# Routing spread over more units and begun during the queries, with its index picking in 16 bits

## The chip, the cores and the metric

One Trainium2 chip, one core. The metric is device time in microseconds of one execution. The kernel before ran three times: 2064.03 us median, 2062.64 lowest, 2065.06 highest.

## The reference

Two layers act on 256 latent tokens of width 1024 (with 256 context tokens in the first). Each layer is a mixer (layer 0: differential attention beside a Fourier mix; layer 1: a chunked gated unit) followed by a PEER block, and the PEER block is what this case is about:

```
q  = (t @ wq).reshape(tokens, 8 heads, 2 halves, 128)
s  = einsum('thsd,hskd->thsk', q, keys)            # 128 keys per head and half
s1, i1 = top_k(s[:, :, 0], 16);  s2, i2 = top_k(s[:, :, 1], 16)
cand   = (s1[..., :, None] + s2[..., None, :]).reshape(tokens, 8, 256)
sc, ci = top_k(cand, 16)
idx    = take_along_axis(i1, ci // 16) * 128 + take_along_axis(i2, ci % 16)
gate   = softmax(sc)
act    = gelu(einsum('td,thkd->thk', t, take(eu, idx)))
out    = einsum('thk,thkd->td', gate * act, take(ev, idx))
```

The experts are 128 x 128 rows of `eu` and `ev` in each layer, 16384 in all. Matrix products, routing included, are in float32 accuracy.

## The kernel before, in words

Everything is unrolled in Python, and the order of each engine's instructions is the order in which the code issues them.

Weights come in units of 128 x 1024 float32 (512 KB), each one DMA on SyncE (class `Stream`, lines 63 to 152, four raw buffers). A unit is split into two parts that sum to it: ScalarE writes the high part `whi` (line 108), VectorE the low part `wlo` (line 114; GpSimd takes a share only outside the PEER block, where `pool_kt` is not 0). There are three pairs of `whi` and `wlo`, and `ahead()` (line 118) issues the split of a coming unit as soon as a pair is free. `lin` (line 227) then multiplies a unit with 256 tokens in 24 matmuls: eight blocks of rows by three terms, high x high, high x low and low x high.

The PEER block (`peer`, from line 956) does not gather experts. It computes all 128 x 128 hidden values in 128 units of `eu` (line 1154), each with `lin` and a GELU into the tile `A` (line 1170), multiplies them by a dense matrix of gates, and then multiplies by all 128 units of `ev` (line 1174). Its stages are in this order:

- the queries: two halves of eight units (line 972). After the eight units of a half, TensorE forms the scores of 128 keys for its eight lists and two tiles of tokens (line 991), and ScalarE copies them into `sc` (line 995). A half holds four heads, two lists for each.
- routing (`routing`, line 999): a generator of small steps, nearly all on VectorE, which ends each step with a `yield`. A list step finds the 16 largest of 128 scores and their positions (lines 1022 to 1026). There are 16 lists for each of two tiles of tokens (`tt`). Per tile there follow the candidate sums (line 1033), eight lists of 112 candidates (lines 1041 to 1045), small integer steps that turn a candidate's position into two positions of 0 to 15 (lines 1048 to 1059), and the picking: for each of the two indices and each half of the heads a comparison with 0 to 15, a multiplication by the sixteen found indices, and a sum over them (lines 1064, 1067, 1070). At the end come the softmax of the gates (lines 1072 to 1080) and the transposes of indices and gates (line 1086).
- the first 64 `eu` units run beside routing. After the instructions of a unit, `run` takes two steps of routing, or one step after every fourth unit (line 1171). At unit 64 whatever is left of it must be done, and its memory is closed and used again (line 1155).
- `eu` units 64 to 127 run beside `gphase(0)`, which builds the dense gates of the first half of the experts from the picked indices (lines 1109 and 1114, two-input VectorE instructions on 16-bit data) and multiplies them into `A` (line 1128). The `ev` units run beside `gphase(1)`.

`rep` is a tile in 16 bits that holds 0 to 127, each twice.

Of the kernel before, what the change touches and what calls it, by code (L numbers as in the profile page):

```python
# [10 lines left out]
F32 = mybir.dt.float32  # L11
# [9 lines left out]
P = 128  # L21
D = 1024
KT = 8
T = 256
# [131 lines left out]
def trunk(ctx, tc, a, out):  # L156
# [799 lines left out]
    def peer(layer, nrm, ln, last):  # L956


        with ExitStack() as px:
# [8 lines left out]
            sc = rp.tile([P, 2, 16, P], F32, name="sc")  # L968
            S.pool_kt = 0

            with tc.tile_pool(name="rq", bufs=2) as rq:
                for half in range(2):
                    qp = rq.tile([P, 8, T], F32, name="qp", bufs=1)
                    ku = rq.tile([P, 8, P], F32, name="ku", bufs=1)
                    A_.dma_start(ku.rearrange("p l k -> p (l k)"), a[f"keys{layer}"][half])
                    if half == 0:
                        late = nrm.products(LATE, lambda l, q, c: A_.activation(qp[:, l, :], q, AF.Identity, bias=c))
                    for l in range(0 if half else LATE, 8):
                        p = mmb()
                        u = S.next()  # L980
                        S.ahead()
                        lin(p, u, thi, tlo)
                        if half == 0 and l == LATE:
                            late()
                            ln.close()
                        A_.activation(qp[:, l, :], p[:, :T], AF.Copy)  # L986
                    for tt in range(2):
                        for g in range(2):
                            p = accb()
                            for j in range(4):  # L990
                                nc.tensor.matmul(p[:, j * P:(j + 1) * P],  # L991
                                                 lhsT=qp[:, g * 4 + j, tt * P:(tt + 1) * P],
                                                 rhs=ku[:, g * 4 + j, :], start=True, stop=True)
                            l0 = half * 8 + g * 4
                            A_.activation(sc[:, tt, l0:l0 + 4, :],
                                          p.rearrange("p (l k) -> p l k", l=4), AF.Copy)
                    S.ahead()

            def routing():
                Vv_ = rp.tile([P, 2, 16, 16], F32, name="V")  # L1000
                I = rp.tile([P, 2, 16, 16], U32, name="I")
                If = rp.tile([P, 2, 16, 16], F32, name="If")
                cand = rp.tile([P, 8, 112], F32, name="cand")
                CV = rp.tile([P, 2, 8, 16], F32, name="CV")
                CI = rp.tile([P, 8, 16], U32, name="CI")
                ab = [rp.tile([P, 8, 16], I32, name=f"ab{i}") for i in range(4)]
                af = [rp.tile([P, 8, 16], F32, name=f"af{i}") for i in range(4)]
                sel = rp.tile([P, 8, 16], F32, name="sel")
                i16 = rp.tile([P, 16], F32, name="i16")
                V.tensor_copy(i16, rep[:, :16, 0])  # L1010
                oh = rp.tile([P, 4, 16, 16], F32, name="oh")
                pick = [rp.tile([P, 2, 8, 16], F32, name=f"pick{i}") for i in range(2)]
                gt = rp.tile([P, 2, 8, 16], F32, name="gt")
                gs = rp.tile([P, 2, 8], F32, name="gs")
                gi = rp.tile([P, 2, 8], F32, name="gi")
                yield
                for tt in range(2):
                    for l in range(16):
                        s = sc[:, tt, l, :]
                        v, i = Vv_[:, tt, l], I[:, tt, l]  # L1020
                        s2 = rp.tile([P, P], F32, name="s2", bufs=2)
                        V.max(v[:, 0:8], s)
                        V.max_index(i[:, 0:8], v[:, 0:8], s)  # L1023
                        V.match_replace(s2, v[:, 0:8], s, NEG)  # L1024
                        V.max(v[:, 8:16], s2)  # L1025
                        V.max_index(i[:, 8:16], v[:, 8:16], s2)  # L1026
                        yield
                    V.tensor_copy(If[:, tt], I[:, tt])
                    Vv = Vv_[:, tt].rearrange("p (h s) k -> p h s k", s=2)
                    Iv = If[:, tt].rearrange("p (h s) k -> p h s k", s=2)  # L1030
                    for lo_, n, nb in ((0, 4, 16), (4, 12, 4)):
                        o = cand[:, :, 0:64] if lo_ == 0 else cand[:, :, 64:112]
                        V.tensor_tensor(
                            o.rearrange("p h (a b) -> p h a b", b=nb),
                            Vv[:, :, 0, lo_:lo_ + n][:, :, :, None].to_broadcast([P, 8, n, nb]),
                            Vv[:, :, 1, 0:nb][:, :, None, :].to_broadcast([P, 8, n, nb]), op=OP.add)
                        yield
                    for h in range(8):
                        s = cand[:, h, :]
                        s2 = rp.tile([P, P], F32, name="s2", bufs=2)  # L1040
                        V.max(CV[:, tt, h, 0:8], s)
                        V.max_index(CI[:, h, 0:8], CV[:, tt, h, 0:8], s)
                        V.match_replace(s2[:, :112], CV[:, tt, h, 0:8], s, NEG)
                        V.max(CV[:, tt, h, 8:16], s2[:, :112])
                        V.max_index(CI[:, h, 8:16], CV[:, tt, h, 8:16], s2[:, :112])
                        yield
                    ci = CI.bitcast(I32)
                    V.tensor_scalar(ab[0], ci, 4, None, op0=OP.logical_shift_right)
                    V.tensor_scalar(ab[1], ci, 15, None, op0=OP.bitwise_and)
                    V.tensor_scalar(ab[2], ci, 2, None, op0=OP.logical_shift_right)  # L1050
                    V.tensor_scalar(ab[3], ci, 3, None, op0=OP.bitwise_and)
                    V.tensor_scalar(sel, ci, 63.5, None, op0=OP.is_gt)
                    yield
                    V.scalar_tensor_tensor(af[2], ab[2], -12.0, ab[0], op0=OP.add, op1=OP.subtract)
                    V.tensor_tensor(af[2], af[2], sel, op=OP.mult)
                    V.tensor_tensor(af[0], ab[0], af[2], op=OP.add)
                    V.tensor_tensor(af[3], ab[3], ab[1], op=OP.subtract)
                    V.tensor_tensor(af[3], af[3], sel, op=OP.mult)
                    V.tensor_tensor(af[1], ab[1], af[3], op=OP.add)
                    yield  # L1060
                    for s in range(2):
                        for hh in range(0, 8, 4):
                            sh = [P, 4, 16, 16]
                            V.tensor_tensor(oh, af[s][:, hh:hh + 4, :, None].to_broadcast(sh),  # L1064
                                            i16[:, None, None, :].to_broadcast(sh), op=OP.is_equal)
                            yield
                            V.tensor_tensor(oh, oh, Iv[:, hh:hh + 4, s, :][:, :, None, :].to_broadcast(sh),
                                            op=OP.mult)
                            yield
                            V.tensor_reduce(pick[s][:, tt, hh:hh + 4], oh, axis=AX.X, op=OP.add)  # L1070
                            yield
                V.tensor_tensor(gt, CV, CV[:, :, :, 0:1].to_broadcast([P, 2, 8, 16]), op=OP.subtract)
                A_.activation(gt, gt, AF.Exp)
                yield
# [8 lines left out]
                for tt in range(2):  # L1083
                    p = gb()
                    for j, src in enumerate((pick[0], pick[1], gt)):
                        nc.tensor.transpose(p[:, j * P:(j + 1) * P],
                                            src[:, tt].rearrange("p h k -> p (h k)"), ident)
                    for j, dst in enumerate((i1T, i2T, gT[0])):
                        A_.activation(dst[:, tt * P:(tt + 1) * P], p[:, j * P:(j + 1) * P], AF.Copy)
                    V.tensor_tensor(gT[1][:, tt * P:(tt + 1) * P], p[:, 2 * P:3 * P],  # L1090
                                    gT[0][:, tt * P:(tt + 1) * P], op=OP.subtract)
                    yield

            def gphase(hf):

# [34 lines left out]
            def run(gen, n):  # L1130
                for _ in range(n):
                    if next(gen, "end") == "end":
                        return True
                return False

            def wsplit(i):
                split_to(thi[:, i % 8, :T], tlo[:, i % 8, :T], A[i // 64][:, i % 64, :])

# [13 lines left out]
            r = routing()  # L1152
            g0 = gphase(0)
            for i in range(128):
                if i == 64:
# [12 lines left out]
                    wsplit(0)  # L1168
                    wsplit(1)
                A_.activation(A[i // 64][:, i % 64, :], p[:, :T], AF.Gelu_apprx_tanh)  # L1170
                run(r, 2 if i % 4 else 1) if i < 64 else run(g0, 1 if i % 32 else 2)
            g1 = gphase(1)
            y = [accb() for _ in range(4)]
            for i in range(128):
# [290 lines left out]
```

## Time and profile before

| | |
|---|---|
| median of three runs | 2064.03 us |
| the profiled execution, its own time | 2063.24 us |
| its span in the trace | 2061.1 us |
| TensorE matmul busy | 1949.5 us, 95% |
| VectorE busy | 1594.1 us, 77% |
| ScalarE busy | 917.8 us, 45% |
| HBM read | 370.14 MB, 180 GB/s over the span |

The profile is one execution, and the span is what lies between its first and last recorded instruction. PE stands for TensorE's matmuls and PEld for its weight loads, DVE for VectorE, ACT for ScalarE, POOL for GpSimd. L114 is line 114 of the kernel. In the lists of instructions, "wlo<-raw,whi" is the tile written and the tiles read. A wait is put down to the instruction whose end came last before it was over. The granted clock is TensorE's, as a part of 2.4 GHz.

### The profile page before, as it was taken

How to read it: one execution, taken by the hardware profiler on the slowest of the kernel's cores; microseconds unless marked ns; L12 is line 12 of the kernel's file. 1: busy time of each engine (PE TensorE's matmuls, PEld its weight loads, DVE VectorE, ACT ScalarE, POOL GpSimd, SP SyncE). 2: the span in 40 equal slices, each digit the busy share in tenths (PEclk: the TensorE clock that was granted, in tenths of full speed). 3: DMA queues.
4: the chain of work that ended last, by engine and by line, in shares of the span. 5: the costliest groups of instructions: out<-in, count | busy, mean ns of one | idle time of the engine just before them, and what ended most of it. 6: DMA issues, size and time to landing. Idle time of an engine off the chain costs nothing.

```text
span 2061.1 us, 35820 instructions
## 1 busy us (share of the span) xinstructions
PE 1949.5 (95%) x14176; PEld 1732.4 (84%) x14176; DVE 1594.1 (77%) x2955; ACT 917.8 (45%) x1460; POOL 160.8 (8%) x133
## 2 busy tenths in 40 slices
PE   7999898889999999999998998989999999999997
PEld 3977898889999977788887998879999987778886
DVE  5797659994888799998888657997677788885554
ACT  4345553344434444444445554334444444444443
POOL 5332300000000000000003610000000000000000
PEclk9999999999999999999999999999999999999998
DMA  7752454455666566678885454545555555556662
GB/s 248 243 174 79 147 162 152 144 160 179 199 189 188 172 204 206 198 252 275 286 277 178 138 185 135 162 141 177 175 164 166 172 170 164 167 172 188 189 189 82
DMA packets 106152, 373.52 MB, mean 181 GB/s; under 512 B 11904, under 2 KB 12544, under 8 KB 105600
## 3 DMA queue, kind: packets, MB, share of 16 engines
q1 hardware_dynamic: 104256, 366.23, 56.3%
q10 hardware_dynamic: 1728, 5.00, 0.7%
q8 instruction: 111, 1.82, 0.4%
q14 instruction: 57, 0.47, 0.1%
HBM read 370.14 MB, written 1.05 MB: 180 GB/s over the span
## 4 chain that ended last, share of the span: by engine, by line
PE 65%; DVE 25%; issue 5%; ACT 3%; POOL 2%; DMA 1%; DVEq 0%; POOLq 0%; ACTq 0%
PE acc L1148 32%; PE acc L233 20%; DVE wlo L114 7%; PE mm L233 5%; PE gg L1125 3%; ACT whi L108 1%; POOL wlo L112 1%; DVE acca L433 1%; DVE I L1026 1%; DVE I L1023 1%; DVE V L1025 1%; DVE s L1024 1%; PE acc L991 1%; DVE oh L1064 1%; DVE o L1109 1%
## 5 line engine op out<-in xcount | busy, mean ns | idle before, releaser
L114 DVE TENSOR_TENSOR wlo<-raw,whi 128x1024 fp32r<-128x1024 f32 (+2 forms) x604 | 718.1, 1190 | 286.6 <-ACT whi L108 284.8
L108 ACT ACTIVATE whi<-raw 128x1024 fp32r<-128x1024 f32 x604 | 635.9, 1055 | 418.2 <-PE acc L1148 333.8
L233 PE MATMUL acc<-thi,wlo 128*128 128x256 f32 (+1 forms) x2016 | 575.1, 286 | 41.7 <-DVE wlo L114 41.7
L233 PE MATMUL acc<-thi,whi 128*128 128x256 f32 (+1 forms) x2016 | 573.1, 285 | 3.6 <-ACT thi L286 3.6
L233 PE MATMUL acc<-tlo,whi 128*128 128x256 f32 (+1 forms) x2016 | 561.6, 282 | 1.3 <-DVE tlo L303 1.3
L233 PEld LDWEIGHTS acc<-thi,wlo 128*128 128x128 f32 x2016 | 383.3, 190 | 53.5 <-DVE wlo L114 53.4
L233 PEld LDWEIGHTS acc<-thi,whi 128*128 128x128 f32 x2016 | 383.0, 190 | 4.0 <-ACT thi L286 4.0
L233 PEld LDWEIGHTS acc<-tlo,whi 128*128 128x128 f32 x2016 | 377.4, 189 | 1.8 <-DVE tlo L303 1.7
L1170 ACT ACTIVATE A<-acc 128x256 f32<-128x256 f32 x240 | 92.3, 385 | 451.6 <-PE acc L233 451.6
L1148 PE MATMUL acc<-whi,thi 128*128 128x512 f32 x1024 | 285.4, 400 | 0.0
L1148 PE MATMUL acc<-whi,tlo 128*128 128x512 f32 x1024 | 281.3, 396 | 0.0
L1148 PE MATMUL acc<-wlo,thi 128*128 128x512 f32 x1024 | 281.1, 395 | 0.0
L1148 PEld LDWEIGHTS acc<-wlo,thi 128*128 128x128 f32 x1024 | 192.6, 188 | 47.6
L1148 PEld LDWEIGHTS acc<-whi,tlo 128*128 128x128 f32 x1024 | 192.6, 188 | 44.8
L1148 PEld LDWEIGHTS acc<-whi,thi 128*128 128x128 f32 x1024 | 187.4, 188 | 39.5
L112 POOL TENSOR_TENSOR wlo<-raw,whi 128x640 fp32r<-128x640 f32 (+1 forms) x62 | 107.6, 1744 | 930.2 <-DVE tlo L303 863.1
L1128 DVE SCALAR_TENSOR_TENSOR A<-gg,A 128x512 f32<-128x512 f32 x128 | 88.4, 691 | 74.7 <-PE gg L1125 74.7
L233 PE MATMUL mm<-tlo,whi 128*128 128x256 f32 (+1 forms) x448 | 127.0, 283 | 2.4 <-DVE tlo L344 2.4
L233 PE MATMUL mm<-thi,whi 128*128 128x256 f32 (+1 forms) x448 | 128.4, 287 | 0.9 <-ACT qp L986 0.9
L233 PE MATMUL mm<-thi,wlo 128*128 128x256 f32 (+1 forms) x448 | 126.3, 282 | 0.0
L485 DVE TENSOR_TENSOR tlo<-A,thi 128x256 fp32r<-128x256 f32 x256 | 107.5, 421 | 0.0
L484 ACT ACTIVATE thi<-A 128x256 fp32r<-128x256 f32 x256 | 102.4, 401 | 0.0
(266 smaller groups left out, 2155.4 us busy)
## 6 DMA issues: line engine op xcount, KB each, us to landing
raw<-in_eu SPq DMA_DIRECT2D x256, 512.0 KB, 3.6
raw<-in_ev SPq DMA_DIRECT2D x256, 512.0 KB, 4.2
raw<-in_ada1t SPq DMA_DIRECT2D x56, 512.0 KB, 4.5
raw<-in_wq SPq DMA_DIRECT2D x32, 512.0 KB, 3.7
ada<-in_ada0t SPq DMA_DIRECT2D x48, 256.0 KB, 4.9
raw<-in_ada0h SPq DMA_DIRECT2D x16, 512.0 KB, 4.4
raw<-in_w_out SPq DMA_DIRECT2D x16, 512.0 KB, 3.6
raw<-in_o_in_u SPq DMA_DIRECT2D x8, 512.0 KB, 4.7
```

What stands on the lines that cost most here:

```text
L108: nc.scalar.activation(hi, r, AF.Copy)
L112: nc.gpsimd.tensor_tensor(lo[:, :a], r[:, :a], hf[:, :a], op=OP.subtract)
L114: nc.vector.tensor_tensor(lo[:, a:], r[:, a:], hf[:, a:], op=OP.subtract)
L233: nc.tensor.matmul(o, lhsT=w[:, k, :], rhs=t[:, k, :n], start=first and j == 0 and i == passes[0], stop=last and j == len(order) - 1 and i ...
L433: V.scalar_tensor_tensor(self.ac, u, cs[:, k, 0:1], self.ac, op0=OP.mult, op1=OP.add)
L484: A_.activation(hi, src, AF.Copy)
L485: V.tensor_tensor(lo, src, hi.bitcast(F32), op=OP.subtract)
L991: nc.tensor.matmul(p[:, j * P:(j + 1) * P], lhsT=qp[:, g * 4 + j, tt * P:(tt + 1) * P], rhs=ku[:, g * 4 + j, :], start=True, stop=True)
L1125: nc.tensor.matmul(pt[:, t, :], lhsT=o2[:, t // 2, :, t % 2], rhs=og[j][:, t // 2, :, t % 2], start=j == 0, stop=j == 1)
L1128: V.scalar_tensor_tensor(av, pt.rearrange("p t i -> p i t"), 1.0 / GSCALE, av, op0=OP.mult, op1=OP.mult)
L1148: nc.tensor.matmul(y[2 * h + tt], lhsT=w[a_][:, tt * P:tt * P + P], rhs=e[b_][:, 512 * h:512 * h + 512], start=i == 0 and n == 0, stop=i = ...
L1170: A_.activation(A[i // 64][:, i % 64, :], p[:, :T], AF.Gelu_apprx_tanh)
```

## The change

Three things are changed, all in `peer`.

- `routing()` is defined ahead of the queries and started in them: after each of the eight units of the second half of the queries one step is taken. The list steps are put in another order for it: first the eight lists of the first half of the queries for both tiles of tokens, then the eight of the second half.
- After each of the first 64 `eu` units one step is taken in place of two or one. The number of steps falls: the first empty step goes, the two candidate sums share a step, the small integer steps share one, and picking takes three steps for each index and tile in place of six.
- Picking works on all eight heads at once, in 16 bits. The found indices are copied to `If` as 16-bit numbers, each twice, once per tile of tokens. The comparison (against `rep`), the multiplication and the sums write 16-bit tiles in which two neighbouring choices are the innermost pair. The sum over sixteen is three halving additions and a fourth that writes 32 bits.

```diff
-            def routing():
...
+                If = rp.tile([P, 16, 16, 2], F16, name="If")
...
+                af = [rp.tile([P, 8, 16], F16 if i < 2 else F32, name=f"af{i}") for i in range(4)]
...
+                oh = rp.tile([P, 64, 16, 2], F16, name="oh")
...
+                for l0 in (0, 8):
+                    for tt in range(2):
+                        for l in range(l0, l0 + 8):
+                            s = sc[:, tt, l, :]
...
+                            V.max_index(i[:, 8:16], v[:, 8:16], s2)
+                            yield
                 for tt in range(2):
...
-                    V.tensor_copy(If[:, tt], I[:, tt])
+                    V.tensor_copy(If, I[:, tt, :, :, None].to_broadcast([P, 16, 16, 2]))
...
-                        for hh in range(0, 8, 4):
-                            sh = [P, 4, 16, 16]
-                            V.tensor_tensor(oh, af[s][:, hh:hh + 4, :, None].to_broadcast(sh),
-                                            i16[:, None, None, :].to_broadcast(sh), op=OP.is_equal)
-                            yield
-                            V.tensor_tensor(oh, oh, Iv[:, hh:hh + 4, s, :][:, :, None, :].to_broadcast(sh),
-                                            op=OP.mult)
-                            yield
-                            V.tensor_reduce(pick[s][:, tt, hh:hh + 4], oh, axis=AX.X, op=OP.add)
-                            yield
+                        sh = [P, 64, 16, 2]
+                        V.tensor_tensor(oh, af[s].rearrange("p h (k j) -> p (h k) j", j=2)[:, :, None, :].to_broadcast(sh),
+                                        rep[:, None, 0:16, :].to_broadcast(sh), op=OP.is_equal)
+                        yield
+                        o4 = oh.rearrange("p (h k) b j -> p h k (b j)", h=8)
+                        V.tensor_tensor(o4, o4, Iv[:, :, s][:, :, None, :].to_broadcast([P, 8, 8, 32]), op=OP.mult)
+                        yield
+                        for n in (8, 4, 2):
+                            V.tensor_tensor(oh[:, :, 0:n], oh[:, :, 0:n], oh[:, :, n:2 * n], op=OP.add)
+                        V.tensor_tensor(pick[s][:, tt].rearrange("p h (k j) -> p (h k) j", j=2),
+                                        oh[:, :, 0], oh[:, :, 1], op=OP.add)
+                        yield
...
+            r = routing()
+            with tc.tile_pool(name="rq", bufs=2) as rq:
...
                         A_.activation(qp[:, l, :], p[:, :T], AF.Copy)
+                        if half:
+                            run(r, 1)
...
-                run(r, 2 if i % 4 else 1) if i < 64 else run(g0, 1 if i % 32 else 2)
+                run(r, 1) if i < 64 else run(g0, 1 if i % 32 else 2)
```

## Rows read from the trace of the kernel before

**Rows 1.** The page: busy time of each engine, and the chain by engine
```profile
PE 1949.5 (95%) x14176; PEld 1732.4 (84%) x14176; DVE 1594.1 (77%) x2955; ACT 917.8 (45%) x1460; POOL 160.8 (8%) x133
...
PE 65%; DVE 25%; issue 5%; ACT 3%; POOL 2%; DMA 1%; DVEq 0%; POOLq 0%; ACTq 0%
```

**Rows 2.** Windows: length; PE, PEld, DVE, ACT, POOL busy; granted clock, DMA share, GB/s
```profile
262.70:289.60 26.90, 26.90 (x230) 26.90 (x230) 9.81 (x8) 13.25 (x22) 0.00 (x0) 1.00 0.59 179
...
289.60:511.00 221.40, 198.59 (x1598) 192.65 (x1598) 184.74 (x513) 93.23 (x143) 0.00 (x0) 0.99 0.50 155
...
462.00:464.00 2.00, 2.00 (x12) 2.00 (x11) 1.23 (x1) 0.05 (x1) 0.00 (x0) 0.50 0.64 205
...
913.00:1048.00 135.00, 135.00 (x585) 109.08 (x585) 116.28 (x159) 66.23 (x97) 0.00 (x0) 1.00 0.85 282
```

**Rows 3.** Waits from 289 to 465 us: who for whom, us, times, longest
```profile
PEld acc L233 <- DVE wlo L114: 26.3, 27, 1.4
```

**Rows 4.** Timeline of DVE: start, duration, then engine, line, operation, tiles
```profile
306.56 1.21 DVE L114 TENSOR_TENSOR wlo<-raw,whi 128x1024 fp32r<-128x1024 f32 x1
307.69 0.29 DVE L1022 MAX8 V<-sc 128x8 f32<-128x128 f32 x1
309.27 1.21 DVE L114 TENSOR_TENSOR wlo<-raw,whi 128x1024 fp32r<-128x1024 f32 x1
...
313.55 1.21 DVE L114 TENSOR_TENSOR wlo<-raw,whi 128x1024 fp32r<-128x1024 f32 x1
```

**Rows 5.** Timeline of PE at units 0 and 48; the two x384 rows are the chain's
```profile
289.22 0.37 PE L233 MATMUL acc<-thi,whi 128*128 128x256 f32 x1
...
460.16 0.30 PE L1086 MATMUL gg<-ident,gt 128*128 128x128 f32 x1 [2.17 <-DVE gt L1077]
...
461.17 0.41 PE L233 MATMUL acc<-thi,whi 128*128 128x256 f32 x1
...
463.09 0.41 PE L233 MATMUL acc<-thi,whi 128*128 128x256 f32 x1
...
464.91 0.36 PE L233 MATMUL acc<-thi,whi 128*128 128x256 f32 x1
...
465.15 45.74 PE acc L233 x384
...
1245.88 0.37 PE L233 MATMUL acc<-thi,whi 128*128 128x256 f32 x1
...
1420.31 45.75 PE acc L233 x384
```

**Rows 6.** Groups of DVE by form, 240 to 720 us: count, busy us, mean ns
```profile
L1109 DVE TENSOR_TENSOR o<-rep,i2T 128x1024 f16<-128x1024 f16 x34 | 23.2, 682 | 0.0
L1109 DVE TENSOR_TENSOR o<-rep,i1T 128x512 f16<-128x512 f16 x34 | 14.3, 420 | 0.0
L1067 DVE TENSOR_TENSOR oh<-oh,If 128x1024 f32<-128x1024 f32 x8 | 9.8, 1222 | 0.1
L1064 DVE TENSOR_TENSOR oh<-af,i 128x1024 f32<-128x1024 f32 x8 | 9.8, 1221 | 0.1
L1070 DVE TENSOR_REDUCE pick<-oh 128x64 f32<-128x1024 f32 x8 | 9.7, 1216 | 0.1
...
L1055 DVE TENSOR_TENSOR af<-af,sel 128x128 f32<-128x128 f32 x2 | 0.6, 292 | 0.1
...
L1028 DVE CAST If<-I 128x256 f32<-128x256 uint32 x2 | 0.6, 287 | 0.0
```

**Rows 7.** Timeline of DVE: the first small integer step and the `wlo` behind the last
```profile
349.17 0.23 DVE L1048 TENSOR_SCALAR ab<-CI 128x128 int32<-128x128 int32 x1
...
352.69 1.22 DVE L114 TENSOR_TENSOR wlo<-raw,whi 128x1024 fp32r<-128x1024 f32 x1
```

**Rows 8.** Timeline of ACT and of DVE in units 48 to 63
```profile
468.04 0.39 ACT L1170 ACTIVATE A<-acc 128x256 f32<-128x256 f32 x1 [1.29 <-PE acc L233]
...
469.40 1.23 DVE L114 TENSOR_TENSOR wlo<-raw,whi 128x1024 fp32r<-128x1024 f32 x1 [1.40 <-ACT whi L108]
```

More of the change, by code (lines that the diff above doesn't have):

```diff
@@ L969, in peer @@
             S.pool_kt = 0
[L971 to L997, printed above, removed]
             def routing():
@@ L1001, in routing @@
                 I = rp.tile([P, 2, 16, 16], U32, name="I")
-                If = rp.tile([P, 2, 16, 16], F32, name="If")
+                If = rp.tile([P, 16, 16, 2], F16, name="If")
                 cand = rp.tile([P, 8, 112], F32, name="cand")
@@ L1006, in routing @@
                 ab = [rp.tile([P, 8, 16], I32, name=f"ab{i}") for i in range(4)]
-                af = [rp.tile([P, 8, 16], F32, name=f"af{i}") for i in range(4)]
+                af = [rp.tile([P, 8, 16], F16 if i < 2 else F32, name=f"af{i}") for i in range(4)]
                 sel = rp.tile([P, 8, 16], F32, name="sel")
-                i16 = rp.tile([P, 16], F32, name="i16")
-                V.tensor_copy(i16, rep[:, :16, 0])
-                oh = rp.tile([P, 4, 16, 16], F32, name="oh")
+                oh = rp.tile([P, 64, 16, 2], F16, name="oh")
                 pick = [rp.tile([P, 2, 8, 16], F32, name=f"pick{i}") for i in range(2)]
@@ L1015, in routing @@
                 gi = rp.tile([P, 2, 8], F32, name="gi")
-                yield
-                for tt in range(2):
[L1018 to L1026, printed above, removed]
-                        yield
-                    V.tensor_copy(If[:, tt], I[:, tt])
+                for l0 in (0, 8):
+                    for tt in range(2):
+                        for l in range(l0, l0 + 8):
+                            s = sc[:, tt, l, :]
+                            v, i = Vv_[:, tt, l], I[:, tt, l]
+                            s2 = rp.tile([P, P], F32, name="s2", bufs=2)
+                            V.max(v[:, 0:8], s)
+                            V.max_index(i[:, 0:8], v[:, 0:8], s)
+                            V.match_replace(s2, v[:, 0:8], s, NEG)
+                            V.max(v[:, 8:16], s2)
+                            V.max_index(i[:, 8:16], v[:, 8:16], s2)
+                            yield
+                for tt in range(2):
+                    V.tensor_copy(If, I[:, tt, :, :, None].to_broadcast([P, 16, 16, 2]))
                     Vv = Vv_[:, tt].rearrange("p (h s) k -> p h s k", s=2)
-                    Iv = If[:, tt].rearrange("p (h s) k -> p h s k", s=2)
+                    Iv = If.rearrange("p (h s) k j -> p h s (k j)", s=2)
                     for lo_, n, nb in ((0, 4, 16), (4, 12, 4)):
@@ L1052, in routing @@
                     V.tensor_scalar(sel, ci, 63.5, None, op0=OP.is_gt)
-                    yield
                     V.scalar_tensor_tensor(af[2], ab[2], -12.0, ab[0], op0=OP.add, op1=OP.subtract)
@@ L1061, in routing @@
                     for s in range(2):
-                        for hh in range(0, 8, 4):
-                            sh = [P, 4, 16, 16]
-                            V.tensor_tensor(oh, af[s][:, hh:hh + 4, :, None].to_broadcast(sh),
-                                            i16[:, None, None, :].to_broadcast(sh), op=OP.is_equal)
-                            yield
-                            V.tensor_tensor(oh, oh, Iv[:, hh:hh + 4, s, :][:, :, None, :].to_broadcast(sh),
-                                            op=OP.mult)
-                            yield
-                            V.tensor_reduce(pick[s][:, tt, hh:hh + 4], oh, axis=AX.X, op=OP.add)
-                            yield
+                        sh = [P, 64, 16, 2]
[9 more added lines that the diff above has]
+                                        oh[:, :, 0], oh[:, :, 1], op=OP.add)
+                        yield
                 V.tensor_tensor(gt, CV, CV[:, :, :, 0:1].to_broadcast([P, 2, 8, 16]), op=OP.subtract)
@@ L1092, in routing, with run @@
                     yield
+            def run(gen, n):
+                for _ in range(n):
+                    if next(gen, "end") == "end":
+                        return True
+                return False
+            r = routing()
+            with tc.tile_pool(name="rq", bufs=2) as rq:
+                for half in range(2):
+                    qp = rq.tile([P, 8, T], F32, name="qp", bufs=1)
+                    ku = rq.tile([P, 8, P], F32, name="ku", bufs=1)
+                    A_.dma_start(ku.rearrange("p l k -> p (l k)"), a[f"keys{layer}"][half])
+                    if half == 0:
+                        late = nrm.products(LATE, lambda l, q, c: A_.activation(qp[:, l, :], q, AF.Identity, bias=c))
+                    for l in range(0 if half else LATE, 8):
+                        p = mmb()
+                        u = S.next()
+                        S.ahead()
+                        lin(p, u, thi, tlo)
+                        if half == 0 and l == LATE:
+                            late()
+                            ln.close()
+                        A_.activation(qp[:, l, :], p[:, :T], AF.Copy)
+                        if half:
+                            run(r, 1)
+                    for tt in range(2):
+                        for g in range(2):
+                            p = accb()
+                            for j in range(4):
+                                nc.tensor.matmul(p[:, j * P:(j + 1) * P],
+                                                 lhsT=qp[:, g * 4 + j, tt * P:(tt + 1) * P],
+                                                 rhs=ku[:, g * 4 + j, :], start=True, stop=True)
+                            l0 = half * 8 + g * 4
+                            A_.activation(sc[:, tt, l0:l0 + 4, :],
+                                          p.rearrange("p (l k) -> p l k", l=4), AF.Copy)
+                    S.ahead()
             def gphase(hf):
@@ L1128, in mult_in @@
                 V.scalar_tensor_tensor(av, pt.rearrange("p t i -> p i t"), 1.0 / GSCALE, av, op0=OP.mult, op1=OP.mult)
[L1130 to L1134, printed above, removed]
             def wsplit(i):
@@ L1150, in y_mult @@
                                              start=i == 0 and n == 0, stop=i == 127 and n == 2)
-            r = routing()
             g0 = gphase(0)
```

## The prediction, made before the changed kernel was timed

> **What bounds the kernel now.** I read the page's shares first, then the busy time by stage, then the waits of one stage, then single instructions. TensorE is busy for 95% of the span and VectorE for 77%, and the chain that ended last runs through TensorE for 65% and VectorE for 25% [rows 1]. So a quarter of the time is set by VectorE somewhere, and the stages say where. The first 64 `eu` units are that place: in layer 0 TensorE is busy for 198.6 of 221.4 us there and VectorE for 184.7 [rows 2]. In the second half of the queries, just before, the picture is the reverse: TensorE 26.9 of 26.9 us, VectorE 9.8 [rows 2]. The waits of the first stage name the releaser: TensorE's weight loads wait 27 times, 26.3 us in all, for `wlo`, the low half of a unit's weights [rows 3]. `wlo` is itself short; it stands on VectorE behind the routing steps.
>
> Starts on VectorE show the exchange rate [rows 4]. `wlo` at 306.56 hands over to a list at 307.69, so it occupies 1.13 us; the next `wlo` starts at 309.27, so a list (five calls, eight instructions) occupies 1.58 us. A unit with one list thus occupies VectorE for 2.71 us; the next one, with two lists, for 4.28 us (309.27 to 313.55). TensorE needs 45.74 us for the last 16 of the 64 units, which have no routing beside them: 2.86 us each [rows 5]. One list fits under a unit, two do not, and three units in four now take two steps.
>
> The lost time follows. Layer 0: unit 0 starts at 289.22, unit 48 at 464.91, so 48 units take 175.7 us where 48 x 2.86 = 137.2 would do: 38.5 us lost. Layer 1: 1245.88 to 1420.07 (the chain's 1420.31 less the 0.24 us by which layer 0's two readings of unit 48 differ), 174.2 us, 37.0 lost [rows 5]. Together 75.5 us, 3.7% of the run, and it is the most that the change can give: units 48 to 63 already run at TensorE's pace.
>
> **The change, part by part.** *Fewer steps per unit.* Routing has 69 steps after the change (32 lists, 2 x 16 of candidates and picking, 5 at the end). Eight run in the queries, 61 in units 0 to 60, one each. Before there were 86, at 1.75 per unit, done at unit 48 or 49. So the 16 idle units at the end are now used, and three units are left before the first user of the indices at unit 64.
>
> *Eight lists in the second half of the queries.* VectorE there gets 9.8 + 8 x 1.58 = 22.4 us of work in 26.9 us. Per query that is 2.71 us under 2.86 us: cost nothing, covered by TensorE with 0.15 us a query to spare. The lists need scores of the first half, which ScalarE copies out as the half begins; the first list stands behind the first `wlo` of the new half, so only that one could wait, in slack. Without the cover each would cost up to its 1.58 us, 25 us in two layers. The added program order puts the lists ahead of a later `wlo` only; no DMA is issued and none is moved, and the weight loads on SyncE are paced by the splits as before.
>
> *Picking in 16 bits.* Now a half of the heads takes compare, multiply and reduce at 1.22 us each over 1024 elements, so both halves of one index take 7.32 us, and four of these per layer 29.3 us [rows 6]. After, one index takes a compare and a multiply over 2048 16-bit elements, then sums of 1024, 512, 256 and 128. A 16-bit two-input instruction of the same broadcast form takes 0.682 us at 1024 and 0.420 us at 512 [rows 6]: 0.262 us per 512 and 0.158 us fixed. That gives 1.21 + 1.21 + 0.68 + 0.42 + 0.29 us; the last sum writes 32-bit and is priced as the 128-element row, 0.29. Sum 4.10 us, 16.4 us per layer, 12.9 less. Upper bound: all of it at the 32-bit slope (1.221 less 0.292 us over 896 elements, 1.04 ns each), 2.28 + 2.28 + 1.22 + 0.69 + 0.43 + 0.29 = 7.2 us, no gain on VectorE. I take the low value because the nearest rows have the same element type and the same inner pair. A price below the low value is excluded as far as the rows go: both 16-bit rows lie on that slope.
>
> *Small edits.* The cast to `If` writes 512 elements instead of 256: between its 0.287 us now and 0.69 us by the 32-bit slope, I take 0.6, so 0.6 us more per layer. The two index steps become one of eleven small instructions; from their first start to the next step they now span 3.52 us with one `wlo` inside [rows 7], 0.66 us over a unit. The two candidate sums (512 and 384 elements, 0.69 and 0.56 us by the 32-bit slope) become one step with the cast: 1.85 us, and with `wlo` 0.12 us over a unit. Candidate lists are 112 wide, so no longer than 128-wide ones.
>
> *Does an over-long step stall TensorE?* With TensorE at its pace, a unit ends and its activation starts at 468.04; the split released by it starts on VectorE at 469.40 and lasts 1.23 [rows 8]. Three weight buffers exist, so this is the split for the unit that starts two units later, at about 468.0 + 5.7 = 473.7. Slack: 473.7 - 470.6 = 3.1 us. The index step's 0.66 us, and even a multiply at the 32-bit bound (2.28 + 1.13 - 2.86 = 0.55), go into that and are won back at 0.15 us or more a unit. Cost nothing.
>
> *What is late next.* VectorE's work in the 64 units becomes 184.7 - 12.9 + 0.6 - 12.6 = 159.8 us, under 64 x 2.86 = 183.0 us. So TensorE is. What is left over its floor: the transposes at the end of routing (six small matmuls, before the first `g` step), and the exponential that ScalarE runs between two activation-table changes. Now TensorE waits 2.17 us for `gt` there and then ran at the lower clock, 0.50 of 2.4 GHz in 462 to 464 [rows 5, 2], inside the 38.5. After, one empty step with a whole unit behind it separates `gt` from the transposes, so I keep 1.5 us per layer, between 0.5 (the matmuls alone) and 5 (wait and lower clock as now: 464.91 less 460.16 is 4.75 us for a 2.86 us unit, 1.9, with 2.2 of waiting and some for the second group).
>
> The Trainium skill's page "TensorE: Matmul & The Clock Gate", Part 1, says that the clock falls to its lower level after idle time, at a moment that does not hang on where the kernel's work begins. This case's row agrees on the order (the wait of 2.17 us, then 0.50). By that rule the lower level goes with the wait, and 0.5 us a layer is kept: 1989.5 us. By the row alone, with the wait kept, it is 5 a layer: 1998.5 us.
>
> **Sum.** 75.5 - 2 x 1.5 = 72.5 us less. The profiled execution took 2063.24 us, 0.8 under the median of 2064.03: 1990.7 on its scale, 1991.5 on the median's. I predict **1991 us**. Its own range is 1986 (nothing kept, and a us of spread) to 2001 (5 us kept per layer and a few stalled units).
>
> **The rivals.**
> *VectorE still binds in part.* The margin per list unit is 0.15 us, and at each unit VectorE also waits for ScalarE's high half. For it: the trace shows no stretch with just one list per unit. Against: a 2.71 us unit is measured, with its hand-overs, and the slack is a unit long. If handing over costs 0.3 us on each of 64 list units and 32 others that are as full, it is 96 x 0.15 = 14 us; with picking at the 32-bit bound some 5 us more per layer. Time 2003 to 2020, taken as 2010.
> *The lists delay the queries.* If the lists wait at the front of VectorE's queue (for scores, or because scores are tracked as one tile so that readers and writers of its two halves wait for each other), the `wlo` behind them is late: up to 25 us as above, time about 2005 to 2016. Against: the first half's scores are out by the time the second half's first split is.
> *Slower: the clock.* TensorE loses its rests in these stages and is granted the lower level, 1.2 GHz, in them. At 0.50 the matmuls followed each other at 0.213 us (461.17 to 463.09, nine of them) [rows 5], against 2.86 / 24 = 0.119, so a unit would cost 24 x 0.094 = 2.3 us more. The change turns into a loss when more than 72.5 / 2.3 = 32 of the 128 units run so; at half of them the time is 1991 + 64 x 2.3 = 2138. For it: the clock does move in this stage. Against: it fell after TensorE had waited, and through 135 us of full work (913 to 1048) it stayed at 1.00 [rows 2].
> *The change does nothing*, because transfers or ScalarE hold the units at the old pace. Against: units 48 to 63 run at 2.86 us with the same loads, and the core moved 282 GB/s in 913 to 1048 against 179 in the queries [rows 2]. Time 2060.
>
> **How the numbers follow.** Forecast 0.74, VectorE in part 0.14, delayed queries 0.06, clock 0.03, nothing 0.03 (of it 0.02 within the bound and 0.01 slower). A change under 0.2%, 4 us, can't be told from none. The range for 8 in 10 runs from 1984 to 2010. Faster 0.94, same 0.02, slower 0.04.
>
> **What would show it.** Right: activations of units 0 to 63 at 2.86 us throughout, the waits of TensorE's weight loads for `wlo` down from 27 to a few, VectorE idle before each `wlo` for ScalarE, both stages near 184 us, queries still 26.9 us. Wrong: gaps at unit starts in the list units (VectorE binds), second-half queries longer than 26.9 us, 2048-element picking near 2.3 us, or a granted clock under 1.00 in the stage. The forecast fails as a whole if TensorE still waits for `wlo` in most units.

## The result, and the profile after

The changed kernel takes 2001.39 us (median of four runs, 2000.04 to 2002.35); the kernel before, run beside it, 2063.34 us. The ratio is 0.9698, with a 95% interval of 0.9681 to 0.9715: 62 us faster. The forecast was 1991 us, with a range of 1984 to 2010.

The page of the kernel after gives the busy times and the chain by engine. VectorE's part of the chain falls from 25% to 11%, TensorE's rises from 65% to 80% [rows 1].

```profile
PE 1930.1 (97%) x14176; PEld 1725.3 (86%) x14176; DVE 1574.9 (79%) x2953; ACT 918.4 (46%) x1460; POOL 160.5 (8%) x133
...
PE 80%; DVE 11%; issue 3%; ACT 3%; POOL 2%; DMA 1%; DVEq 0%; POOLq 0%; ACTq 0%
```

Windows of the kernel after, the second half of the queries and the first 64 `eu` units of layer 0 (length; busy time of PE, PEld, DVE, ACT, POOL; granted clock, DMA share, GB/s). TensorE is busy for all of both. The second window is 184.6 us long; the 221.4 us of [rows 2] reach some 6 us past unit 63 (see the part on the prediction), so the table further down compares like with like. In the first, VectorE went from 9.8 to 21.5 us and TensorE lost nothing.

```profile
262.80:289.40 26.60, 26.60 (x228) 26.60 (x227) 21.50 (x72) 13.16 (x21) 0.00 (x0) 1.00 0.58 179
...
289.40:474.00 184.60, 184.60 (x1552) 184.60 (x1551) 160.22 (x442) 91.48 (x140) 0.00 (x0) 1.00 0.59 180
```

The waits of the second window, longest first. The line of [rows 3], TensorE's weight loads behind `wlo` with 26.3 us, is gone; VectorE now waits for ScalarE.

```profile
ACT A L1172 <- PE acc L233: 92.8, 61, 1.5
DVE wlo L114 <- ACT whi L108: 14.9, 15, 3.8
DVE gT L1062 <- ACT gT L1061: 2.3, 2, 1.2
ACT sc L1099 <- PE acc L1095: 0.6, 2, 0.3
```

The chain of the kernel after in layer 1's stage (start, us, what, and its instructions). Sixty units run without one other link, 171.61 us or 2.86 us each. Only the two groups of transposes come between units, 0.33 us each.

```profile
1209.89 3.57 PE acc L1095 x32
1213.46 171.61 PE acc L233 x1440
1385.07 0.33 PE gg L1058 x3
1385.40 2.85 PE acc L233 x24
1388.25 0.33 PE gg L1058 x3
```

VectorE's groups in the first window of units, by form (count, busy us, mean ns), answer to [rows 6]. Compare and multiply over 2048 elements take 1.218 us, the four sums 0.684, 0.426, 0.294 and 0.294, the wider cast 0.420.

```profile
L1037 DVE TENSOR_TENSOR oh<-oh,If 128x2048 f16<-128x2048 f16 x4 | 4.9, 1218 | 0.0
L1033 DVE TENSOR_TENSOR oh<-af,rep 128x2048 f16<-128x2048 f16 x4 | 4.9, 1218 | 0.0
...
L1040 DVE TENSOR_TENSOR oh<-oh 128x1024 f16<-128x1024 f16 x4 | 2.7, 684 | 0.0
...
L1040 DVE TENSOR_TENSOR oh<-oh 128x512 f16<-128x512 f16 x4 | 1.7, 426 | 0.1
...
L1040 DVE TENSOR_TENSOR oh<-oh 128x256 f16<-128x256 f16 x4 | 1.2, 294 | 0.1
L1041 DVE TENSOR_TENSOR pick<-oh 128x128 f32<-128x128 f16 x4 | 1.2, 294 | 0.1
...
L999 DVE CAST If<-I 128x512 f16<-128x512 uint32 x2 | 0.8, 420 | 0.0
```

The Trainium skill's page "VectorE: DVE Perf Modes", section "The perf-mode tier table (the rule you actually need)", gives 1224 ns for a two-input instruction over 2048 bf16 elements, and 2293 ns in fp32. This trace agrees with 1218 ns for the first, in the kernel's own 16-bit type, and experiment e5 below with 2.28 us for the second.

For what follows, the stage is measured from the first activation of an `eu` unit (unit 0) to that of unit 64, from their starts in the timelines:

| kernel | layer 0, us | layer 1, us |
|---|---|---|
| before | 215.8 | 214.3 |
| after | 183.8 | 183.7 |

That is 32.0 and 30.6 us, 62.6 of the 63.2 us by which the spans differ (2061.1 less 1997.9). The rest lies outside: the stretches between the stages move by more than that from one profile to the next (last section).

### The profile page after: what moved, and what is told of

Its sections match the earlier page's. It is cut to its first block, busy times and chain, and to the rows that moved or that the text cites. A ratio compares the mean times of both kernels' runs of the same rounds, so it can differ in the third digit from the quotient of the medians.

```text
span 1997.9 us, 35816 instructions
## 1 busy us (share of the span) xinstructions
PE 1930.1 (97%) x14176; PEld 1725.3 (86%) x14176; DVE 1574.9 (79%) x2953; ACT 918.4 (46%) x1460; POOL 160.5 (8%) x133
## 4 chain that ended last, share of the span: by engine, by line
PE 80%; DVE 11%; issue 3%; ACT 3%; POOL 2%; DMA 1%; DVEq 0%; POOLq 0%; ACTq 0%
PE acc L233 34%; PE acc L1151 33%; PE mm L233 5%; PE gg L1134 3%; DVE wlo L114 3%; POOL wlo L112 1%; DVE acca L433 1%; ACT whi L108 1%; PE acc L1095 1%; DVE o L1118 1%; DVE z L723 1%; DMA raw<-in_ada0h 1%; DVE og L1123 1%; DVE e L746 1%; DVE x L488 0%
## 5 line engine op out<-in xcount | busy, mean ns | idle before, releaser
L233 PE MATMUL acc<-thi,wlo 128*128 128x256 f32 (+1 forms) x2016 | 568.1, 283 | 0.4 <-DVE wlo L114 0.4
```

The costliest lines, as they stand in the source:

```text
L233: nc.tensor.matmul(o, lhsT=w[:, k, :], rhs=t[:, k, :n], start=first and j == 0 and i == passes[0], stop=last and j == len(order) - 1 and i ...
```

## The experiments

Two theories were set against each other. S: the stage costs what VectorE's work exceeds TensorE's pace by, unit by unit, so the *spreading* decides. W: VectorE *work* saved (16 bits) or moved away (into the queries) is what gives time. Stage times are per layer, layer 0 first; the floor is 183.8 us.

**e1: the changed kernel at the old pace.**

```diff
-                run(r, 1) if i < 64 else run(g0, 1 if i % 32 else 2)
+                run(r, 2 if i % 4 else 1) if i < 64 else run(g0, 1 if i % 32 else 2)
```

> The changed kernel with only the pace of routing in the eu units put back: two steps a unit, one after every fourth. Theory S (what the stage costs is set by how VectorE's work lies over the units; TensorE waits when the work of successive units exceeds 2.86 us by more than the 3.1 us of slack): 61 steps fall into 35 units, some 88 us of routing and 35 x 1.13 us of splits against 35 x 2.86 = 100 us, so some 25 us a layer are lost again: about 2050 us, 2040 to 2058. Theory W (the gain is VectorE work that was saved or moved to the queries; its sum stays under TensorE's 183 us): no change, 2001 to 2006 us.

Measured: 2060.43 us, ratio to before 0.9982 (0.9972 to 0.9992); stage 212.9 and 212.9 us. Lighter picking and the early start, without the spreading, are worth 3.5 us out of 62 (2.9 and 1.4 us by the stages). S is right in kind, 10 us short in size and 2 us outside its range; W is wrong. The wait is back (who for whom, us, times, longest; 289 to 480 us):

```profile
PEld acc L233 <- DVE wlo L114: 26.5, 23, 1.7
```

**e2: the kernel before, only spread.**

```diff
-                run(r, 2 if i % 4 else 1) if i < 64 else run(g0, 1 if i % 32 else 2)
+                run(r, 2 if i % 8 in (0, 3, 6) else 1) if i < 64 else run(g0, 1 if i % 32 else 2)
```

> The kernel before with only the pace changed: its 86 steps spread over the 64 units, eleven steps in eight units; 32-bit picking and the start after the queries stay. Theory S: VectorE's occupied time, about 168 us less 49 splits plus 64 splits, is 185 us for 64 units against TensorE's 183; the lists at 1.375 a unit come to 3.30 us a unit for 23 units, so some 8 to 12 us a layer stay lost of 32: 2015 us, 2005 to 2025. Theory W: none of the work is saved or moved, so the loss stays: 2050 to 2063 us.

Measured: 2015.82 us, 0.9764 (0.9748 to 0.9780); stage 190.6 and 190.6 us. This one line gives 48 of the 62 us. S holds, W falls. TensorE's weight loads still wait for `wlo`, but six times:

```profile
PEld acc L233 <- DVE wlo L114: 6.0, 6, 1.2
```

**e3: the kernel before, only the 16-bit picking** (`If`, `af`, `oh` and the three picking steps as in the diff ahead of the prediction, everything else as before).

```diff
-                oh = rp.tile([P, 4, 16, 16], F32, name="oh")
+                oh = rp.tile([P, 64, 16, 2], F16, name="oh")
...
-                        for hh in range(0, 8, 4):
+                        sh = [P, 64, 16, 2]
```

> The kernel before with only the picking changed to 16 bits and the tree (three steps for each index and tile in place of six); pace and start stay. Theory S: the stage is bound by VectorE until routing ends, so the 12.9 us a layer of VectorE time saved come out in full, less 0.3 for the larger cast: 2063 - 25 = 2038 us, 2034 to 2042. Theory W gives the same 25 us. A rival that the 16-bit form runs slower in place (2.28 us for 2048 elements) gives 2060 us, but the changed kernel's trace has 1.22 us already.

Measured: 2065.15 us (ten runs, 2062.5 to 2072.1), 1.0014 (1.0001 to 1.0027); stage 216.5 and 216.5 us. Both theories missed by 27 us: 12.5 us of VectorE work a layer less gave nothing. The activations show the stall at routing's end at unit 40 (8.84 us after the one before) where the kernel before has it at unit 47 (6.98 us). Picking has twelve steps fewer, so at an unchanged pace the work lies on seven units fewer, and each unit not used takes its room away. That led to a third theory, R: while routing runs, the loss is its VectorE time less the room it is given, and the room is 2.86 - 1.13 = 1.73 us per unit used.

**e9: the test of R.** 16-bit picking in the kernel before with an empty step behind each picking step, so that the work of e3 lies on 49 units.

```diff
                         yield
+                        yield
```

> The 16-bit picking in the kernel before, as in the run before it, but with an empty step behind each picking step, so that routing keeps 86 steps and 49 units at the old pace. Theory R (while routing runs, the loss per layer is VectorE's routing time less 1.73 us, that is 2.86 less 1.13, for each unit it is spread over; work saved pays only when the number of units stays): routing 100.3 us less 49 x 1.73 = 84.8 leaves 15.5 us where the kernel before has 27.8: 12.3 us a layer less, 2039 us, 2033 to 2046. Rival (the stage is bound by steps a unit, whatever they weigh, so lighter picking doesn't pay): 2060 to 2066 us.

Measured: 2042.59 us, 0.9892 (0.9875 to 0.9908); stage 204.4 and 204.4 us. Twelve empty steps a layer make e3 22.6 us faster, inside R's range of 2033 to 2046, and the rival's 2060 to 2066 is out. But R's hit is in part luck. Of the 12.1 us a layer by which the stages of e3 and e9 differ, 5.8 are the stall at routing's end, where ScalarE in e3 waits 4.47 us for `gt` (first row) and in e9 not at all; R does not contain it. In the units before, e9 loses 6.3 us less, where R names 12.3. The wait for `wlo` falls too (second and third row, who for whom, us, times, longest; e3 from 289 to 435 us, then e9 from 289 to 470):

```profile
438.59 0.42 ACT L1073 ACTIVATE gt<-gt 128x256 f32<-128x256 f32 x1 [4.47 <-DVE gt L1072]
```

```profile
PEld acc L233 <- DVE wlo L114: 26.1, 25, 1.4
```

```profile
PEld acc L233 <- DVE wlo L114: 19.5, 18, 1.4
```

**e4: the changed kernel without the steps in the queries.**

```diff
-                        if half:
-                            run(r, 1)
...
-                run(r, 1) if i < 64 else run(g0, 1 if i % 32 else 2)
+                run(r, 1 if i % 8 else 2) if i < 64 else run(g0, 1 if i % 32 else 2)
```

> The changed kernel without the steps in the queries: all 69 steps lie in the 64 eu units, one each and a second one in every eighth. Theory S: VectorE gets 160.2 + 8 x 1.58 = 172.9 us against 183.0; the lists at 1.125 a unit come to 2.91 us, 0.05 over for 28 units, 1.4 us, which fits in the slack: 2001 us, 2000 to 2005. Theory W: the work moved to the queries comes back, 12.6 us a layer: up to 2027 us.

Measured: 2002.36 us, 0.9701 (0.9685 to 0.9717); stage 183.8 and 183.8 us, as in the changed kernel, whose interval it shares. With the other two parts in place the early start gives nothing that can be told.

**e5: the changed kernel with 32-bit picking.**

```diff
-                oh = rp.tile([P, 64, 16, 2], F16, name="oh")
+                oh = rp.tile([P, 64, 16, 2], F32, name="oh")
```

(`If` and `af` likewise.)

> The changed kernel with its picking in 32 bits, in the same three steps and the same tree. Theory S: compare and multiply become 2.28 us each, the sums 1.22, 0.69, 0.43 and 0.29 us: 12 us a layer more on VectorE, 172 of 183 us. Locally a picking step is 0.55 to 0.75 us over a unit, 3.8 us for the six in a row, and 0.6 before them: 4.4 us against 3.1 of slack, so at most 1.3 us for each tile of tokens and 2.6 a layer: 2003 us, 2001 to 2007. Theory W: the 12 us a layer come back: 2025 us.

Measured: 2009.81 us, 0.9745 (0.9729 to 0.9762); stage 187.5 and 187.8 us. W is wrong by 15 us, S by 3 at its upper end. VectorE's group of comparisons (count, busy us, mean ns) shows the price of one:

```profile
L1033 DVE TENSOR_TENSOR oh<-af,rep 128x2048 f32<-128x2048 f32 x4 | 9.1, 2285 | 0.0
```

1.4 us of the 3.7 are lost at units 41 and 42, where the first picking outruns the slack, the rest at the end. ScalarE's timeline there (start, us, what, wait): it holds the table change for the exponential at 453.70, waits 2.83 us for `gt`, which stands behind the late picking on VectorE, and 6.8 us go by from the end of one split (451.29) to the start of the next (458.14).

```profile
450.24 1.05 ACT L108 ACTIVATE whi<-raw 128x1024 fp32r<-128x1024 f32 x1
453.30 0.38 ACT L1172 ACTIVATE A<-acc 128x256 f32<-128x256 f32 x1 [2.01 <-PE acc L233]
453.70 1.28 ACT L1045 ACT_TABLE_LOAD   x1
457.81 0.42 ACT L1045 ACTIVATE gt<-gt 128x256 f32<-128x256 f32 x1 [2.83 <-DVE gt L1044]
458.14 1.05 ACT L108 ACTIVATE whi<-raw 128x1024 fp32r<-128x1024 f32 x1
```

In the kernel after the same step has no wait in it:

```profile
452.63 0.39 ACT L1172 ACTIVATE A<-acc 128x256 f32<-128x256 f32 x1 [1.53 <-PE acc L233]
453.04 1.28 ACT L1045 ACT_TABLE_LOAD   x1
454.33 0.42 ACT L1045 ACTIVATE gt<-gt 128x256 f32<-128x256 f32 x1
454.66 1.04 ACT L108 ACTIVATE whi<-raw 128x1024 fp32r<-128x1024 f32 x1
```

**e6 and e7: how much room VectorE has left.** One more product in each of the first 64 units, of 256 elements in e6 and of 512 in e7, whose edit stands here (`dz` is a tile set to ones once, ahead of the queries).

```diff
+                if i < 64:
+                    V.tensor_tensor(dz[:, 0, :512], dz[:, 1, :512], dz[:, 1, :512], op=OP.mult)
```

> The changed kernel with one more VectorE instruction in each of the first 64 eu units, a product of 256 32-bit elements that nothing reads (0.42 us long, about 0.34 from start to start). Theory S: VectorE's 160 us become 182 of 183; list units become 3.05 us, 0.19 over, 4.6 us for 24 of them against 3.1 of slack, and candidate lists 0.1 over: 1 to 5 us a layer lost: 2006 us, 2002 to 2012. A rival in which VectorE has much more room than its busy time shows: 2001 us. A rival in which it binds already (hand-overs not seen as busy): every unit pays 0.34 us, 2001 + 2 x 22 = 2045 us.

> The same with 512 elements (0.69 us long, about 0.61 from start to start). Theory S: VectorE's 160 us become 199 against 183, less 3.1 of slack, and gaps that VectorE can't fill: 13 to 22 us a layer: 2035 us, 2027 to 2046. Much more room: 2001 to 2010 us. Binding already: 2001 + 2 x 39 = 2079 us.

Measured: e6 2012.03 us, 0.9756 (0.9740 to 0.9772), stage 188.6 and 188.8; e7 2041.95 us, 0.9900 (0.9883 to 0.9916), stage 203.8 and 204.0. 0.34 us more per unit costs 10.6 us, 0.61 costs 40.6: the kink that S puts between them is there. In size S is 6 and 7 us low, with e6 at the very end of its range; both rivals are off by more. VectorE's timeline of e7 (start, us, what) shows what a list unit then takes: 1.12 + 0.61 + 1.58 = 3.31 us from split to split, and the activations of units 10 to 26 follow at 3.30 us.

```profile
314.19 1.21 DVE L114 TENSOR_TENSOR wlo<-raw,whi 128x1024 fp32r<-128x1024 f32 x1
315.31 0.69 DVE L1176 TENSOR_TENSOR dz<-dz 128x512 f32<-128x512 f32 x1
315.92 0.29 DVE L992 MAX8 V<-sc 128x8 f32<-128x128 f32 x1
...
317.50 1.21 DVE L114 TENSOR_TENSOR wlo<-raw,whi 128x1024 fp32r<-128x1024 f32 x1
```

**e8: the changed kernel without routing's work.**

```diff
-                for l0 in (0, 8):
...
+                for t in (pick[0], pick[1], gt):
+                    V.memset(t, 1.0)
+                for _ in range(67):
+                    yield
```

> The changed kernel without routing's work: lists, candidates, picking and the softmax of the gates are left out (indices and gates are constants), the transposes stay where they are. Theory S: routing is hidden in full but for the transposes, which stay, so only a few tenths a layer go: 2001 us, 1999 to 2002. If routing still costs something that the trace doesn't show as a wait (clock, memory, ScalarE's two table changes), the time falls under 1998 us, and by so much.

Measured: 2002.57 us, 0.9705 (0.9689 to 0.9721); stage 183.8 and 183.8 us. VectorE is busy for 79 us in it in place of 160, and TensorE for all of it as before (same columns as the windows above):

```profile
293.00:476.50 183.50, 183.50 (x1543) 183.50 (x1542) 78.99 (x66) 87.73 (x137) 0.00 (x0) 1.00 0.60 181
```

The whole time is 0.6 us above the range that was expected; the stage is that of the changed kernel. So routing is hidden in full but for its transposes, which stay in this kernel. The changed kernel is at this stage's floor: no other way to do routing's VectorE work can win time in this stage. A faster version would have to be looked for in other stages, which was not tried.

**e10: 32-bit picking and the late start together**, the edits of e4 and e5 in one.

```diff
-                oh = rp.tile([P, 64, 16, 2], F16, name="oh")
+                oh = rp.tile([P, 64, 16, 2], F32, name="oh")
...
-                        if half:
-                            run(r, 1)
```

> The changed kernel with 32-bit picking and without the steps in the queries, its 69 steps over 61 units. Theory R: routing 88 + 12.6 + 12 = 112.6 us less 61 x 1.73 = 105.5 leaves 7 us a layer, 1 to 2 more at the exponential: 2018 us, 2012 to 2024. Rival (each part has its price of its own and they add, 1 us for the late start and 8.4 for 32 bits): 2011 us, 2009 to 2012.

Measured: 2025.96 us, 0.9810 (0.9794 to 0.9827); stage 195.9 and 196.2 us. Undone alone, the parts cost 1 and 8 us; undone together, 24.6. The parts share one budget, so their prices don't add. R's direction holds, its size is 2 us short even of its upper end. The waits of e10 show the mechanism of e5 again, larger:

```profile
PEld acc L233 <- DVE wlo L114: 6.9, 8, 2.7
...
ACT gt L1045 <- DVE gt L1044: 5.0, 1, 5.0
...
PEld acc L233 <- ACT whi L108: 1.7, 1, 1.7
```

**All of them in R's terms.** Routing's VectorE time in the stage before is what VectorE did from the split at 293.72 to the end of the first subtraction of `gT` (line 1090) at 461.78, 168.1 us, less 1.8 of waits and 48 splits of 1.13: 112 us. The 16-bit picking takes 12.5 off it (4 x 3.19 less 2 x 0.13 for the cast), the queries take 8 x 1.58 = 12.6. Room is 1.73 us a unit. The loss measured is the stage of layer 0 less 183.8. The last column is the part of it at the exponential: the five steps between activations from the late one on, less 5 x 2.86 us, less the 0.7 us that remain of the same in the kernel after.

| kernel | routing, us | units | R: loss, us | measured, us | at the exponential, us |
|---|---|---|---|---|---|
| before | 112 | 49 | 27 | 32.0 | 3.9 |
| e3 | 99.5 | 42 | 27 | 32.7 | 5.8 |
| e9 | 99.5 | 49 | 15 | 20.6 | 0.0 |
| e1 | 87 | 35 | 26 | 29.1 | 3.8 |
| e2 | 112 | 62.5 | 4 | 6.8 | 0.0 |
| e10 | 112 | 61 | 6 | 12.1 | 5.2 |
| e5 | 99 | 61 | 0 | 3.7 | 1.5 |
| e6 | 108 | 61 | 2 | 4.8 | 0.1 |
| e7 | 124 | 61 | 19 | 20.0 | 1.3 |
| e4 | 99.5 | 61 | 0 | 0.0 | 0.0 |
| after | 87 | 61 | 0 | 0.0 | 0.0 |

R orders all of them but e7 and e9 and is 1 to 6 us low wherever there is a loss. The last column says where. In the kernel before, e1, e3 and e10 the shortfall is at the exponential: ScalarE waits there for `gt`, 2.6, 3.9, 4.5 and 5.0 us, and its splits wait behind it. What these four and e7 lose elsewhere (28.1, 25.3, 26.9, 6.9 and 18.7 us) is R's figure to within about 1 us. In e9, e2, e6 and e5 the shortfall of 2 to 6 us lies in the units: room that a light stretch leaves beyond the slack is lost (e9 runs at 2.86 us from unit 19 to 28, while it loses before and after). e2 and e10 have the same work in R's terms and nearly the same units, but e10 is 10.1 us slower: its fewer steps are longer, and what it loses at the exponential, 5.2 us a layer that e2 doesn't lose, accounts for all of it.

## Why the prediction was right, and where it was 10 us off

*What bounds the kernel.* Right. The stage was bound by VectorE's queue in front of `wlo`, and e8 shows that nothing else of routing costs time.

*The lost time, 75.5 us.* This term failed; it was mis-sized. The matmul at 464.91 was taken as the start of unit 48, from 16 units that the chain's 45.74 us hold [rows 5]. The units were not counted. ScalarE's groups of the kernel before in the windows 289 to 465.1 and 1245 to 1420.2 us, one row each (count, busy us, mean ns, idle before), count them:

```profile
L1170 ACT ACTIVATE A<-acc 128x256 f32<-128x256 f32 x50 | 19.2, 384 | 101.2 <-PE acc L233 101.2
...
L1170 ACT ACTIVATE A<-acc 128x256 f32<-128x256 f32 x50 | 19.2, 384 | 101.0 <-PE acc L233 101.0
```

Fifty units had run, so the 16 units were 50 to 65, the last two of them past unit 63. The floor to subtract was 50 x 2.86 = 143.0, the loss 175.7 - 143.0 = 32.7 and 174.2 - 143.0 = 31.2: 63.9 us, not 75.5. The difference is four units, two a layer.

*What is kept, 2 x 1.5 us.* Too high by 1.7: the transposes take 0.33 us twice a layer and no wait is left (units 57 and 58 are activated 4.37 and 1.35 us after the ones before them in layer 1, but that is ScalarE's table change, and TensorE's chain above has no gap there). 63.9 - 1.3 = 62.6 us is what the stages gave. With the count right the sum would have been 2063.2 - 62.6 = 2000.6 us against 2000.04 for the profiled execution.

*One list per unit fits.* Right: 60 units at 2.86 us, and lists in the queries at no cost. VectorE's timeline after, in the queries (start, us, what), has the next split 2.86 us after the last, with the list between them:

```profile
270.24 1.23 DVE L114 TENSOR_TENSOR wlo<-raw,whi 128x1024 fp32r<-128x1024 f32 x1
271.39 0.29 DVE L992 MAX8 V<-sc 128x8 f32<-128x128 f32 x1
...
273.10 1.23 DVE L114 TENSOR_TENSOR wlo<-raw,whi 128x1024 fp32r<-128x1024 f32 x1
```

But the early start was described as if it mattered, and e4 shows that the 64 units alone would have carried it.

*Picking at 4.10 us an index.* Right: 1.218 + 1.218 + 0.684 + 0.426 + 0.294 + 0.294 = 4.13. The cast was priced at 0.6 and takes 0.42.

*The slack of 3.1 us.* Right in size (e5's first picking, with 4.4 us of excess, loses 1.4). That a multiply at the 32-bit bound would cost nothing was reckoned for one alone, which was not tried: six such steps in a row and `gt` behind them cost 8.4 us in e5.

*VectorE's 159.8 us, TensorE next.* TensorE is next, right. That 160.2 us were measured is in part luck: the 184.7 us of [rows 2] come from a window to 511 us, while unit 64, 14 units after 464.91, starts near 505. To there VectorE is busy for 180.6 us (columns of [rows 2]), and the same sum would have given 155.7. Where the other 4.5 us come from was not looked for.

```profile
289.60:505.00 215.40, 192.59 (x1541) 186.69 (x1541) 180.63 (x507) 90.51 (x138) 0.00 (x0) 0.99 0.50 154
```

*The rivals.* VectorE in part did not occur; with 0.34 us more per unit it would have (e6). The queries were not delayed. The clock stayed at 1.00 through the stage, without the fall that followed the wait of 2.17 us [rows 5, 2]. The Trainium skill's page "TensorE: Matmul & The Clock Gate", Part 1, has the clock fall after idle time; layer 0 of the kernel before agrees. But "wait and lower clock as now" holds for layer 0 alone. In layer 1 the same wait of 2.17 us was followed by the full clock (timeline of PE, then windows, columns of [rows 2]). The 15 matmuls at some 0.21 us in place of 0.12 in layer 0 are the 1.4 us that it loses more than layer 1 (32.0 and 30.6 us).

```profile
1416.81 0.30 PE L1086 MATMUL gg<-ident,gt 128*128 128x128 f32 x1 [2.17 <-DVE gt L1077]
```

```profile
1415.00:1419.00 4.00, 2.19 (x19) 2.23 (x20) 3.29 (x7) 3.69 (x8) 0.00 (x0) 1.00 0.39 135
```

The total came out inside the range of 1984 to 2010 because that left room for stalls, and just past the sum's own 1986 to 2001; it was an error of counting that used the room up, not a stall.

## What to carry to other kernels

Work hidden beside a paced engine has a budget for each step of that engine (here 1.73 us of VectorE a unit, with about a unit of slack): spread it until every step fits, before making it lighter. Lighter work taken at the same number of steps per unit just ends sooner and gained nothing here (e3); undoing two parts that share a budget costs more than the sum of each (e10). Look at the end of the hidden work too: an instruction that waits for it on another engine holds everything behind it (5.8 us a layer in e3). When a floor is subtracted, count the units between the two marks in the trace.

## What was not expected of the hardware

Stretches that the edits don't touch differ between the profiles, of which each kernel has one. Unit 0 of layer 0 is activated at 290.8 us (e6) to 295.4 us (e8), and units 64 to 127 of layer 0 take 201.4 us in some kernels (before, after, e2, e6 to e8) and 202.9 in the others, though the edits act on the units before. The second is the clock. In each of the kernels with 202.9 us the granted clock is down in one stretch of some 4 us in these units, in the others in none. The same wait of 1.7 us of TensorE for `og` lies before the stretch in e4, where it falls, and in the kernel after, where it does not; their windows, e4 first (columns of [rows 2]):

```profile
581.00:585.00 4.00, 4.00 (x22) 4.00 (x22) 3.43 (x6) 0.00 (x0) 0.00 (x0) 0.57 0.53 145
```

```profile
580.00:584.00 4.00, 4.00 (x42) 4.00 (x38) 3.43 (x6) 0.77 (x2) 0.00 (x0) 1.00 0.47 162
```

The first goes with the clock at least in part: from 30 to 60 us it was granted at 0.89 in the kernel after (unit 0 at 292.5) and at 0.72 in e8 (295.4); their windows, in this order:

```profile
30.00:60.00 30.00, 22.78 (x129) 16.48 (x130) 24.07 (x40) 15.07 (x25) 22.26 (x20) 0.89 0.61 192
```

```profile
30.00:60.00 30.00, 23.77 (x115) 17.87 (x116) 23.82 (x38) 14.91 (x24) 22.10 (x20) 0.72 0.59 193
```

In the profiles e8's unit 0 is 2.9 us later than the changed kernel's, more than the 1.2 us by which e8, with less work, is slower in the medians. Differences of a few us between whole times are therefore read as effects of an edit only where the stages show them. What decides whether the clock falls after such a wait was not tried, nor whether it goes with the build or with the single execution.
